# The low parts of all weights made by adding transfers of GpSimd's queue instead of VectorE subtractions

## The chip, the cores and the metric

The kernel runs on one core of one Trainium2 chip, as one program. The metric is the device time of an execution in microseconds. Engines are named TensorE (PE in rows), VectorE (DVE), ScalarE (ACT), GpSimd (POOL) and SyncE (SP, which only issues transfers here).

## The reference

One block of a network over 1024 positions of width 1024, all in float32. With `mod = silu(c) @ w_ada + b_ada` split in six:

```
h    = rmsnorm(x) * (1 + sc1) + sh1
proj = h @ w_in            # convolution branch (a_val, a_gate), z, xbc, dt
u    = silu(layernorm(causal_dwconv(a_val * sigmoid(a_gate), 31 taps))) ; out_a = u @ w_a_out
y    = ssd_scan(silu(causal_dwconv(xbc, 4 taps)), dt) ; y = rmsnorm_groups(y * silu(z)) ; out_b = y @ w_b_out
g_a, g_b = sigmoid(h @ w_gate + b_gate)
x    = x + gt1 * ((g_a * out_a + g_b * out_b) @ w_o)
h2   = rmsnorm(x) * (1 + sc2) + sh2
x    = x + gt2 * ((silu(f_gate) * f_val) @ w_down)     # f_gate, f_val: causal_dwconv(h2 @ w_up, 3 taps)
out  = rmsnorm(x)
```

## The kernel before

Channels lie on the 128 partitions and positions along the free dimension, so a tile of activations is 128x1024. Every large product is made in three: each operand is held as a high part (rounded to the type fp32r, in which TensorE takes it) and a low part (what the rounding left), and the sum is high x high + high x low + low x high. In `dense` these are L203 (`whi` with the high activations), L204 (`whi` with the low activations) and L206 (`wlo` with the high activations). A weight block is 128x1024 floats, 512 KB; it serves one product of 128 channels by 1024 positions, 48 matmuls of 512 columns. In the output projection a block serves one half of the positions only, 24 matmuls.

The program is a list of jobs. A job with a weight block takes it from `fetched`; ahead of each job `fetch_ahead` orders the blocks of this job and of the two after it. `fetch` (L165) loads the block into `raw` (two buffers, the transfer issued on SP), and `split` (L105) makes the two parts: ScalarE copies `raw` into `whi` with the rounding (L107), VectorE subtracts `whi` from `raw` into `wlo` (L98). `whi` and `wlo` have three buffers each, so the parts of block i+2 are made once the products of block i-1 are over. The first two blocks, gates 14 and 15, are loaded apart (`raw_ga`), and the four of the last group lie in buffers of their own. There are 178 blocks: 56 of `w_in`, 44 of `w_up`, 22 of `w_down`, 16 each of `w_gate`, `w_b_out` and `w_o` (each of the 8 of `w_o` twice), 8 of `w_a_out`.

In time: the inputs arrive and h is built (to 33 us); the gates, the projections of the first norm and the SSD scan in four groups (to 980 us), where VectorE also runs the 31 taps of the convolution as background work; the branch outputs `bo` and `ao` (to 1262 us), with four of the six parts of `mod` summed in the background (`ada_acc`, VectorE steps over loaded blocks of `w_ada`, whose transposes on TensorE stand in a fixed place, L234); the output projection (to 1353 us); the up- and down-projections; the last norm.

A scheduler orders the instructions of each engine from the program's order and its own estimate of when operands are ready; on the chip each engine runs its list in order, and semaphores hold an instruction until its operands and buffers are free. GpSimd runs only the powers of the norms (`rs`, L132 and L302) and issues no transfer.

Of the kernel before, what the change touches and what calls it, by code (L numbers as in the profile page):

```python
# [7 lines left out]
F32 = mybir.dt.float32  # L8
F32R = mybir.dt.float32r
AF = mybir.ActivationFunctionType  # L10
ALU = mybir.AluOpType
AX = mybir.AxisListType
PSUM = bass.MemoryType.PSUM
DRAM = bass.MemoryType.DRAM

P = 128
# [16 lines left out]
EPS = 1e-6  # L33
EPS_SSM = 1e-5

# what runs beside the SSD pieces of each group: pairs of products of the convolution branch, gates
FILL = ("ppgp", "pgpgg", "pgpgg", "pggg")

# their order: fill, z products, pieces (a, b: tokens, s: states, p: pairs of heads)
ORDER = ("fafbfspfppfpafbsfppzpzpzz",) * 3 + ("fafbspfppfpabfsppzpzpzz",)  # L40

_COLS = [
# [15 lines left out]
def block_kernel(ctx: ExitStack, tc: tile.TileContext, x, xT, par, cst, dtp, w_ada, w_in, w_dt,  # L58
                 w_gate, w_a_out, w_b_out, w_o, w_up, w_down, out):
    nc = tc.nc  # L60
    V, S, G, PE = nc.vector, nc.scalar, nc.gpsimd, nc.tensor
# [44 lines left out]
    def split(src, hi, lo):  # L106
        S.copy(hi, src)  # L107
        sub(lo, src, hi.bitcast(F32))
# [12 lines left out]
        return pars[:, o + i:o + i + n]  # L121

    def rstd_a(ps, scale, eps, name):
        """From a row ps that is the same on every partition: diagonal blocks of rsqrt(scale * ps + eps)."""
        n = ps.shape[-1] // P
        junk = small.tile([P, 4, P], F32, tag="junk", name=f"{name}_junk")[:, 0:n]
        mul(junk, ps.rearrange("p (a b) -> p a b", a=n), idb[:, 0:n])
        ms = small.tile([P, 4], F32, tag="ms", name=f"{name}_ms")[:, 0:n]
        V.tensor_reduce(ms, junk, AX.X, ALU.add)
        V.tensor_scalar(ms, ms, scale, eps, ALU.mult, ALU.add)  # L130
        rs = small.tile([P, 4], F32, tag="rs", name=f"{name}_rs")[:, 0:n]
        G.tensor_tensor(rs, ms, neghalf[:, 0:n], ALU.pow)  # L132
        dg = small.tile([P, 4, P], F32, tag="junk", name=f"{name}_dg")[:, 0:n]
        mul(dg, idb[:, 0:n], rs.unsqueeze(2).broadcast_to([P, n, P]))
        return dg

    def rstd_b(dg, name):
        """PSUM tile [P, 512]: the row on every partition."""
        dg = dg.rearrange("p a b -> p (a b)")
        ps = small_ps(f"{name}_row")[:, 0:dg.shape[-1]]  # L140
        PE.matmul(ps, ones, dg, start=True, stop=True)
        return ps
# [4 lines left out]
            PE.matmul(ps, ones, q, start=i == 0, stop=i == len(sqs) - 1)  # L147
        return ps

    # ---------------- weights: raw block -> high and low parts, loaded ahead of their use  # L150
    jobs = []
    fetched = {}

# [9 lines left out]
        return raw  # L163

    def fetch(i, raw=None, tag=None):  # L165
        make = w_tile
        if raw is None:
            ap, tag, make = jobs[i][1:]
            raw = raw_load(ap, tag)
        whi, wlo = make(f"whi_{tag}"), make(f"wlo_{tag}")  # L170
        split(raw, whi, wlo)
        fetched[i] = (whi, wlo)

    def fetch_ahead(i, n=3):
# [16 lines left out]
                fn(fetched.pop(i))  # L191

    def dense(outs, w, xs, w0=0, stride=P, after={}):
        """For each (psum, slice of the positions) in outs: psum = w.T @ xs[:, slice] over all k.
        after[k] is called behind the products of k."""
        whi, wlo = w
        nk = len(xs)
        for k in range(nk):
            a, b = xs[k]
            lh = whi[:, w0 + k * stride:w0 + k * stride + P]  # L200
            ll = wlo[:, w0 + k * stride:w0 + k * stride + P]
            for ps, sl in outs:
                PE.matmul(ps, lh, a[:, sl], start=k == 0, stop=False)  # L203
                PE.matmul(ps, lh, b[:, sl], start=False, stop=False)  # L204
            for ps, sl in outs:
                PE.matmul(ps, ll, a[:, sl], start=False, stop=k == nk - 1)  # L206
            if k in after:
                after[k]()
# [1 line left out]
    def dense2(ps, w, xs, **kw):  # L210
        dense([(ps[:, hsl(q)], hsl(q)) for q in range(2)], w, xs, **kw)

    # ---------------- modulation, first norm
    mod = cpool.tile([P, NMOD * KD], F32, name="mod")
    sc = cpool.tile([P, KD], F32, name="sc")
    th = cpool.tile([P, KD], F32, name="th")
# [20 lines left out]
            add(m, m, col("b_ada", q * KD + 4 * hh, 4))  # L237

    def row_sum(ps, col_k, raw, k):
        """One term of the sums over k; the four groups of 32 partitions hold k modulo 4."""  # L240
        kp = 32 * (k % 4)
        PE.matmul(ps[kp:kp + 32], col_k.broadcast_to([P, 32]), raw, start=k < 4, stop=k >= 4)

    def rows_to_cols(ps, dst, rows):
        """The rows ps, summed over the four groups of partitions, as columns."""
        n = dst.shape[-1]
        S.copy(rows, ps)
        pt = small_ps("rows_t")[:, 0:n * P]
        for j in range(n):
            PE.transpose(pt[:, j * P:(j + 1) * P], rows[:, j * P:(j + 1) * P], ident)  # L250
        V.tensor_reduce(dst, pt.rearrange("p (a k r) -> p a k r", a=n, k=4)[:, :, :, 0], AX.X, ALU.add)
# [66 lines left out]
    ada_rows_end(pq, 1)  # L318
    A1 = cpool.tile([P, KD], F32, name="A1")
    stt(A1, mod[:, KD:2 * KD], 1.0, col("norm1_g", 0, KD), ALU.add, ALU.mult)  # L320
    # h without the shift, for the first gates; the shift enters their bias
    halve("b_gate", 0, 16)
    for k in range(KD):
        if k < 2:
# [47 lines left out]
    cud = dram.tile([KD, P, T], F32, name="cud")  # L372
    job(first_gates_job)

    # ---------------- all projections of the first norm; SSD branch; convolution branch up to its norm
    dt, acum, mid, cd, dte = (s1.tile([P, NC, NH], F32, name=n) for n in ("dt", "acum", "mid", "cd", "dte"))
    acd = dram.tile([NH, T], F32, name="acd")

# [1 line left out]
    dts = {}  # L380

    def dt_product():
        # the sums over k lie on four groups of 32 partitions, k modulo 4
        dt_ps = dense_ps("dt_ps")
        for k in range(KD):
            kp = 32 * (k % 4)
            for h in range(2):
                PE.matmul(dt_ps[kp:kp + NH, hsl(h)], wdts[:, k], hf32[:, k, hsl(h)], start=k < 4, stop=k >= 4)
        S.copy(hf32[:, 0], dt_ps)  # L389

    def dt_softplus():
        psx = [small_ps(f"dt_tok{i}") for i in range(2)]
        for c in range(NC):
            PE.transpose(psx[c // 4][:, (c % 4) * P:(c % 4 + 1) * P], hf32[:, 0, c * CL:(c + 1) * CL], ident)
        xv, ev, zv, wv, qv = (hf32[:, 1 + n // 4, 256 * (n % 4):256 * (n % 4) + 256].rearrange(
            "p (c h) -> p c h", c=NC) for n in range(5))
        ea = hf32[:, 2, 512:512 + NH]
        S.activation(ea, dtps[:, 1], AF.Exp)
        for i in range(2):
            V.tensor_reduce(xv[:, 4 * i:4 * i + 4], psx[i].rearrange("p (c k h) -> p c h k", c=4, k=4), AX.X, ALU.add)  # L400
        add(xv, xv, dtps[:, 0].unsqueeze(1).broadcast_to([P, NC, NH]))
        # softplus(x) = max(x, 0) + log1p(e), e = exp(-|x|); log1p(e) = 2 atanh(e / (2 + e))
        stt(ev, xv, -1.0, xv, ALU.mult, ALU.max)
        S.activation(ev, ev, AF.Exp, scale=-1.0)
        V.tensor_scalar(zv, ev, 2.0, None, ALU.add)
        V.reciprocal(wv, zv)
        mul(zv, ev, wv)
        mul(wv, zv, zv)
        V.tensor_scalar(qv, wv, 1.0 / 15, None, ALU.mult)
        for n in (13, 11, 9, 7, 5, 3):  # L410
            stt(qv, qv, 1.0 / n, wv, ALU.add, ALU.mult)
        stt(qv, qv, 1.0, zv, ALU.add, ALU.mult)
        V.tensor_scalar(xv, xv, 0.0, None, ALU.max)
        stt(dt, qv, 2.0, xv, ALU.mult, ALU.add)
        dts["da"] = ev
        stt(ev, dt, -1.0, ea.unsqueeze(1).broadcast_to([P, NC, NH]), ALU.mult, ALU.mult)

    def dt_sums():
        # acum: cumulated log decay counted from the middle of its chunk
        daf = dts["da"].rearrange("p c h -> p (c h)")  # L420
        psa, psb = small_ps("acum_ps"), small_ps("tot_ps")
        PE.matmul(psa[:, 0:256], cums, daf, start=True, stop=True)
# [22 lines left out]
    acb_seq = [(hf, HG * g + q) for g in range(NG) for hf in range(2) for q in range(HG)]  # L445

    def acb_get(i):
        """acum of one head and half of the positions, on every partition."""
        for k in range(i, min(i + 3, len(acb_seq))):
            if k not in acb:  # L450
                hf, h = acb_seq[k]
                acb[k] = env["sp"].tile([P, HT], F32, tag="acb", name=f"acb{hf}_{h}", bufs=4)
                nc.sync.dma_start(acb[k], acd[h:h + 1, hsl(hf)].broadcast_to([P, HT]))
        return acb[i]

    # background work of the vector engine: the 31 taps, spread over the jobs
    bg = []

    def bg_run(n):
# [245 lines left out]
    job(lambda: merge_pools())  # L705
    job(lambda: y_raw(0))

    # ---------------- branch outputs, merge
    def merge_pools():
        sctx.close()  # L710
        env["xp2"] = ctx.enter_context(tc.tile_pool(name="xp2", bufs=8, reuse_waits="tile"))
# [69 lines left out]
            cus.append(t)  # L781

    def layer_norm():
        """Queued as background work."""
        st = {}
        put = lambda f: bg.append((0, f))

# [81 lines left out]
    for m in range(KD):  # L869
        ao_job(m)  # L870

    # output projection, residual
    gt1 = cpool.tile([P, KD], F32, name="gt1")
    A2 = cpool.tile([P, KD], F32, name="A2")
    x2 = []
# [51 lines left out]
        if m < 5:  # L927
            job(lambda m=m: norm2_b(0, 2 * m - 2, 2 * m))

    # ---------------- gated convolutional FFN  # L930
    gt2 = mod[:, 5 * KD:6 * KD]

    def ffn_pool():
# [4 lines left out]
    job(ffn_pool)  # L938

    def up_parts(m, name):  # L940
        """The two halves of a product, and what follows it."""
        def start(w):
            env["ps", m] = dense_ps(f"up_ps{m}")

# [33 lines left out]
        mk(NF + i, "v")  # L978

    def first_tiles(ms):  # L980
        """The first products: the first half of the positions before the second."""
        parts = [up_parts(m, n) for m, n in ms]
        keep = []

# [191 lines left out]
```

## Time and profile before

| | |
|---|---|
| median of 3 runs | 2103.17 us (2100.58 to 2103.53) |
| profiled execution, span from first to last instruction | 2100.7 us (the page gives no other time of it) |
| TensorE busy | 2061.3 us, 98% |
| VectorE busy | 1341.3 us, 64% |
| ScalarE busy | 766.4 us, 36% |
| GpSimd busy | 22.8 us, 1% |
| granted clock of TensorE, mean | 0.994 of 2.4 GHz |
| moved by transfers | 192.37 MB |

The busy time of TensorE counts matmuls in flight; where it is below the length of a stretch, TensorE stood still. Of the other engines, idle time costs nothing as long as nothing waits for them.

### The profile page before, as it was taken

How to read it: one execution, taken by the hardware profiler on the slowest of the kernel's cores; microseconds unless marked ns; L12 is line 12 of the kernel's file. 1: busy time of each engine (PE TensorE's matmuls, PEld its weight loads, DVE VectorE, ACT ScalarE, POOL GpSimd, SP SyncE). 2: the span in 40 equal slices, each digit the busy share in tenths (PEclk: the TensorE clock that was granted, in tenths of full speed). 3: DMA queues.
4: the chain of work that ended last, by engine and by line, in shares of the span. 5: the costliest groups of instructions: out<-in, count | busy, mean ns of one | idle time of the engine just before them, and what ended most of it. 6: DMA issues, size and time to landing. Idle time of an engine off the chain costs nothing.

```text
span 2100.7 us, 23558 instructions
## 1 busy us (share of the span) xinstructions
PE 2061.3 (98%) x9608; PEld 1664.2 (79%) x9608; DVE 1341.3 (64%) x1441; ACT 766.4 (36%) x1163; POOL 22.8 (1%) x28
## 2 busy tenths in 40 slices
PE   6999999999999999999998999999999999999997
PEld 4787787778887887788787888788888888888887
DVE  4658999999669975965886544665434434344356
ACT  5436632564237524753430323342312213122131
POOL 0000000000000000000000000000000000000000
PEclk9999999999999999999999999999999999999999
DMA  8121212232212321317385422211111111111112
GB/s 307 61 73 61 89 53 100 71 110 71 101 51 81 100 101 41 111 70 265 126 283 197 170 100 90 81 51 51 45 46 51 51 50 41 50 51 51 44 37 81
DMA packets 59964, 192.37 MB, mean 92 GB/s; under 512 B 6800, under 2 KB 10256, under 8 KB 59856
## 3 DMA queue, kind: packets, MB, share of 16 engines
q1 hardware_dynamic: 57552, 182.48, 25.5%
q10 hardware_dynamic: 2304, 8.39, 1.1%
q8 instruction: 76, 1.25, 0.2%
q14 instruction: 32, 0.26, 0.0%
HBM read 165.54 MB, written 25.30 MB: 91 GB/s over the span
## 4 chain that ended last, share of the span: by engine, by line
PE 93%; DVE 4%; DMA 2%; ACT 1%; issue 0%; POOL 0%; SPq 0%; POOLq 0%; DVEq 0%; ACTq 0%
PE up_ps L203 8%; PE up_ps L204 8%; PE up_ps L206 8%; PE xbc_ps L203 4%; PE xbc_ps L206 4%; PE xbc_ps L204 4%; PE dn_ps L203 4%; PE dn_ps L206 4%; PE dn_ps L204 4%; PE g_ps L204 3%; PE g_ps L203 3%; PE z_ps L203 3%; PE g_ps L206 3%; PE z_ps L204 3%; PE z_ps L206 3%; PE yd_ps L598 2%
## 5 line engine op out<-in xcount | busy, mean ns | idle before, releaser
L101 DVE SCALAR_TENSOR_TENSOR cu<-u,pars,cu 128x1003 f32<-128x1003 f32 (+18 forms) x240 | 300.5, 1265 | 2.3
L203 PE MATMUL up_ps<-h_hi,whi_up 128*128 128x512 f32 x704 | 274.7, 390 | 0.0
L204 PE MATMUL up_ps<-h_lo,whi_up 128*128 128x512 f32 x704 | 273.9, 389 | 0.0
L206 PE MATMUL up_ps<-h_hi,wlo_up 128*128 128x512 f32 x704 | 220.7, 389 | 0.0
L203 PE MATMUL xbc_ps<-h_hi,whi_in 128*128 128x512 f32 x384 | 153.5, 400 | 1.1 <-ACT hf L389 1.1
L203 PEld LDWEIGHTS up_ps<-h_hi,whi_up 128*128 128x128 f32 x704 | 132.1, 188 | 28.1 <-issue 0.5
L204 PEld LDWEIGHTS up_ps<-h_lo,whi_up 128*128 128x128 f32 x704 | 132.2, 188 | 27.9 <-issue 0.5
L206 PEld LDWEIGHTS up_ps<-h_hi,wlo_up 128*128 128x128 f32 x704 | 132.1, 188 | 27.4
L98 DVE TENSOR_TENSOR wlo_up<-raw_up,whi_up 128x1024 fp32r<-128x1024 f32 x44 | 53.8, 1223 | 151.3 <-ACT whi_up L107 151.0
L204 PE MATMUL xbc_ps<-h_lo,whi_in 128*128 128x512 f32 x384 | 149.7, 390 | 0.0
L107 ACT CAST whi_up<-raw_up 128x1024 fp32r<-128x1024 f32 x44 | 46.3, 1053 | 278.8 <-PE up_ps L204 137.2
L203 PE MATMUL dn_ps<-act_hi,whi_dn 128*128 128x512 f32 (+2 forms) x384 | 146.5, 382 | 1.3 <-DVE up L101 0.9
L204 PE MATMUL dn_ps<-act_lo,whi_dn 128*128 128x512 f32 (+2 forms) x384 | 143.6, 374 | 0.5 <-DVE act_lo L98 0.5
L101 DVE SCALAR_TENSOR_TENSOR x<-dn_ps,mod,x 128x1024 f32<-128x1024 f32 (+2 forms) x64 | 64.8, 1017 | 115.1 <-PE dn_ps L206 115.0
L107 ACT CAST whi_in<-raw_in 128x1024 fp32r<-128x1024 f32 x56 | 58.6, 1047 | 200.9 <-PE xbc_ps L204 72.7
L101 DVE SCALAR_TENSOR_TENSOR up<-up_ps,pars,up 128x1023 f32<-128x1023 f32 x88 | 112.6, 1279 | 14.2 <-ACT up L952 12.7
L206 PE MATMUL dn_ps<-act_hi,wlo_dn 128*128 128x512 f32 (+2 forms) x384 | 121.3, 376 | 0.0
L206 PE MATMUL xbc_ps<-h_hi,wlo_in 128*128 128x512 f32 x384 | 118.4, 390 | 0.0
L98 DVE TENSOR_TENSOR wlo_in<-raw_in,whi_in 128x1024 fp32r<-128x1024 f32 x56 | 68.4, 1221 | 63.6 <-ACT whi_in L107 63.4
L203 PE MATMUL g_ps<-h_hi,whi_ga 128*128 128x512 f32 x256 | 104.7, 409 | 2.0 <-ACT h_hi L328 1.9
L204 PE MATMUL g_ps<-h_lo,whi_ga 128*128 128x512 f32 x256 | 102.3, 400 | 0.0
L203 PE MATMUL bo_ps<-y_hi,whi_bo 128*128 128x512 f32 x256 | 102.1, 400 | 0.0
(263 smaller groups left out, 4122.6 us busy)
## 6 DMA issues: line engine op xcount, KB each, us to landing
raw_in<-in_w_in SPq DMA_DIRECT2D x56, 512.0 KB, 3.5
ada<-in_w_ada SPq DMA_DIRECT2D x48, 512.0 KB, 5.8
raw_up<-in_w_up SPq DMA_DIRECT2D x44, 512.0 KB, 3.4
acb<-acd SPq DMA_DIRECT2D x64, 256.0 KB, 3.5
raw_dn<-in_w_down SPq DMA_DIRECT2D x22, 512.0 KB, 3.4
raw_ga<-in_w_gate SPq DMA_DIRECT2D x16, 512.0 KB, 3.5
gd<-g_t ACTq DMA_DIRECT2D x16, 512.0 KB, 3.3
yd<-xs SPq DMA_DIRECT2D x16, 512.0 KB, 3.7
```

What stands on the lines that cost most here:

```text
L98: V.tensor_tensor(o, a, b, ALU.subtract)
L101: V.scalar_tensor_tensor(o, a, s, b, op0, op1)
L107: S.copy(hi, src)
L203: PE.matmul(ps, lh, a[:, sl], start=k == 0, stop=False)
L204: PE.matmul(ps, lh, b[:, sl], start=False, stop=False)
L206: PE.matmul(ps, ll, a[:, sl], start=False, stop=k == nk - 1)
L598: PE.matmul(psy[e * HD:(e + 1) * HD, i * CL:(i + 1) * CL], xdt[:, i, (2 * j + e) * HD:(2 * j + e + 1) * HD], decs[e][:, i], start=True, st ...
```

## The change

In `fetch` the subtraction of VectorE goes. ScalarE makes a second pass: it writes the negative of the high part into `wlo`. Then GpSimd's queue issues a transfer that adds the weight block to `wlo`, read a second time from DRAM (for the first two blocks from `raw_ga`). All 178 blocks take this way; `split` remains for activations. The rest of the edit takes out comments, which moves the line numbers by two.

```
     def fetch(i, raw=None, tag=None):
-        make = w_tile
+        make, ap = w_tile, None
         if raw is None:
             ap, tag, make = jobs[i][1:]
             raw = raw_load(ap, tag)
         whi, wlo = make(f"whi_{tag}"), make(f"wlo_{tag}")
-        split(raw, whi, wlo)
+        S.copy(whi, raw)
+        S.activation(wlo, whi.bitcast(F32), AF.Copy, scale=-1.0)
+        G.dma_start(wlo, raw if ap is None else ap, accum_op=ALU.add)
         fetched[i] = (whi, wlo)
```

The scheduler gives new orders. On TensorE, at the first product (gates 14 and 15, `g_ps_392` and `g_ps_393`; `ada_ps` are the steps of the shift's sum), before:

```order
L203 MATMUL g_ps_392<-h_hi_343,whi_ga_339 128x512
L203 MATMUL g_ps_393<-h_hi_343,whi_ga_347 128x512
L242 MATMUL ada_ps_0_430<-ada_0_146,sc 32x512
L204 MATMUL g_ps_392<-h_lo_344,whi_ga_339 128x512
L203 MATMUL g_ps_392<-h_hi_343,whi_ga_339 128x512
L204 MATMUL g_ps_392<-h_lo_344,whi_ga_339 128x512
L206 MATMUL g_ps_392<-h_hi_343,wlo_ga_340 128x512 x2
```

and in the changed kernel, the same place on TensorE (the gates are `g_ps_394` and `g_ps_395` there):

```order
L206 MATMUL g_ps_394<-h_lo_345,whi_ga_339 128x512
L244 MATMUL ada_ps_1_433<-ada_0_146,sc 32x512
L244 MATMUL ada_ps_0_432<-ada_1_148,sc 32x512
L244 MATMUL ada_ps_1_433<-ada_1_148,sc 32x512
L205 MATMUL g_ps_395<-h_hi_344,whi_ga_348 128x512
L206 MATMUL g_ps_395<-h_lo_345,whi_ga_348 128x512
L205 MATMUL g_ps_395<-h_hi_344,whi_ga_348 128x512
L206 MATMUL g_ps_395<-h_lo_345,whi_ga_348 128x512
L208 MATMUL g_ps_394<-h_hi_344,wlo_ga_340 128x512 x2
```

The first product with a low part (L206 before, L208 now) has moved back behind the first four products of gate 15 and three more steps of the sum; the four products and one step of gate 14 that stand ahead of these rows are the same.

On ScalarE, in the output projection (`n_q` are the squares for the second norm), before:

```order
L107 CAST whi_o_4_9033<-raw_o_4_9031 128x1024
L899 ACTIVATE n_q_1_9028<-x_1_8932 128x512
L107 CAST whi_o_5_9068<-raw_o_5_9066 128x1024
L899 ACTIVATE n_q_2_9063<-x_2_8934 128x512
L107 CAST whi_o_6_9103<-raw_o_6_9101 128x1024
L899 ACTIVATE n_q_3_9098<-x_3_8936 128x512
```

and in the changed kernel, the same blocks on ScalarE:

```order
L171 CAST whi_o_4_9133<-raw_o_4_9131 128x1024
L901 ACTIVATE n_q_1_9128<-x_1_9030 128x512
L172 ACTIVATE wlo_o_4_9134<-whi_o_4_9133 128x1024
L171 CAST whi_o_5_9169<-raw_o_5_9167 128x1024
L901 ACTIVATE n_q_2_9164<-x_2_9032 128x512
L172 ACTIVATE wlo_o_5_9170<-whi_o_5_9169 128x1024
L171 CAST whi_o_6_9205<-raw_o_6_9203 128x1024
L901 ACTIVATE n_q_3_9200<-x_3_9034 128x512
L172 ACTIVATE wlo_o_6_9206<-whi_o_6_9205 128x1024
```

The negation of each block stands behind the square of the job that ended, not right behind its cast.

## Rows read from the trace of the kernel before

**Rows 1.** The page, busy time of each engine, share of the span, instructions.

```profile
PE 2061.3 (98%) x9608; PEld 1664.2 (79%) x9608; DVE 1341.3 (64%) x1441; ACT 766.4 (36%) x1163; POOL 22.8 (1%) x28
```

**Rows 2.** Busy time by stretches; after POOL: granted clock, DMA share, GB/s.

```profile
0.00:52.00 52.00, 34.53 (x169) 21.55 (x169) 26.03 (x44) 27.14 (x39) 4.72 (x13) 0.93 0.81 311
...
33.00:41.00 8.00, 7.61 (x15) 3.22 (x16) 7.86 (x8) 8.00 (x9) 0.00 (x0) 0.61 1.03 402
...
600.00:900.00 300.00, 300.00 (x1517) 237.38 (x1516) 244.14 (x277) 161.31 (x337) 2.85 (x2) 1.00 0.25 83
...
1100.00:1150.00 50.00, 44.42 (x195) 36.45 (x194) 32.47 (x33) 4.01 (x4) 0.00 (x0) 0.93 0.65 216
...
1117.00:1121.00 4.00, 4.00 (x14) 3.52 (x15) 3.76 (x7) 0.00 (x0) 0.00 (x0) 0.50 0.45 135
...
2050.00:2101.00 51.00, 39.79 (x241) 36.85 (x239) 33.35 (x70) 9.34 (x20) 2.39 (x3) 0.90 0.24 83
```

**Rows 3.** Waits of TensorE: total us, times, longest.

```profile
PE ada_ps L234 <- DVE ada_acc L101: 5.6, 2, 4.8
```

**Rows 4.** Timeline, up-projection: start, us, engine, operation, [idle before <-releaser].

```profile
1464.30 1.05 ACT L107 CAST whi_up<-raw_up 128x1024 fp32r<-128x1024 f32 x1 [4.86 <-PE up_ps L204]
...
1465.39 1.23 DVE L98 TENSOR_TENSOR wlo_up<-raw_up,whi_up 128x1024 fp32r<-128x1024 f32 x1 [7.10 <-ACT whi_up L107]
...
1475.18 1.05 ACT L107 CAST whi_up<-raw_up 128x1024 fp32r<-128x1024 f32 x1 [3.71 <-PE up_ps L204]
...
1487.22 0.61 PE L206 MATMUL up_ps<-h_hi,wlo_up 128*128 128x512 f32 x2
```

**Rows 5.** Timeline, output projection: one block from its cast to its first use.

```profile
1290.12 1.05 ACT L107 CAST whi_o<-raw_o 128x1024 fp32r<-128x1024 f32 x1 [3.86 <-PE o_ps L204]
1291.19 0.63 ACT L899 ACTIVATE n_q<-x 128x512 f32<-128x512 f32 x1
...
1291.20 1.23 DVE L98 TENSOR_TENSOR wlo_o<-raw_o,whi_o 128x1024 fp32r<-128x1024 f32 x1
...
1301.74 0.40 PE L206 MATMUL o_ps<-mix_hi,wlo_o 128*128 128x512 f32 x1
```

**Rows 6.** Timeline, the first product (gate 14).

```profile
31.87 1.22 DVE L98 TENSOR_TENSOR wlo_ga<-raw_ga,whi_ga 128x1024 fp32r<-128x1024 f32 x1
...
32.05 1.15 ACT L328 ACTIVATE h_hi<-hf,A 128x1024 fp32r<-128x1024 f32 x1 [0.47 <-DVE A L101]
...
33.25 1.73 PE L203 MATMUL g_ps<-h_hi,whi_ga 128*128 128x512 f32 x2 [1.91 <-ACT h_hi L328]
...
34.90 1.92 PE L242 MATMUL ada_ps<-ada,sc 128*32 128x512 f32 x2
...
37.77 0.63 PE L204 MATMUL g_ps<-h_lo,whi_ga 128*128 128x512 f32 x1
...
38.19 1.06 PE L206 MATMUL g_ps<-h_hi,wlo_ga 128*128 128x512 f32 x2
```

**Rows 7.** Groups by line, L98 into low parts: count, busy us, mean ns.

```profile
L98 DVE TENSOR_TENSOR wlo_in<-raw_in,whi_in 128x1024 fp32r<-128x1024 f32 x56 | 68.4, 1221 | 63.6 <-ACT whi_in L107 63.4
...
L98 DVE TENSOR_TENSOR wlo_ao<-raw_ao,whi_ao 128x1024 fp32r<-128x1024 f32 x8 | 9.8, 1223 | 26.1 <-ACT whi_ao L107 26.1
```

**Rows 8.** Transfers by issue: count, size, median us from issue to landing.

```profile
raw_up<-in_w_up SPq DMA_DIRECT2D x44, 512.0 KB, 3.4
...
xtok<-in_x SPq DMA_DIRECT2D x8, 512.0 KB, 9.0
...
cu_in<-cud SPq DMA_DIRECT2D x8, 512.0 KB, 10.8
```

**Rows 9.** Timeline, VectorE and TensorE around the wait at 1117 us.

```profile
1106.28 1.22 DVE L98 TENSOR_TENSOR wlo_bo<-raw_bo,whi_bo 128x1024 fp32r<-128x1024 f32 x1
...
1115.62 1.28 DVE L101 SCALAR_TENSOR_TENSOR ada_acc<-ada,sc,ada_acc 128x1024 f32<-128x1024 f32 x1 [3.45 <-DMA ada<-in_w_ada]
...
1116.96 1.97 PE L234 MATMUL ada_ps<-csts,ada_acc 128*128 128x128 f32 x8 [4.80 <-DVE ada_acc L101]
```

## The prediction, made before the changed kernel was run

> **What bounds the kernel now.** I read the busy totals of the page first: TensorE is busy 2061.3 of 2100.7 us, VectorE 64%, ScalarE 36%, GpSimd 1% [rows 1]. So only 39.4 us of the span are not TensorE's, and no removal of VectorE work can be worth more than the part of them that VectorE causes. The table by stretches says where they lie [rows 2]: 17.5 us in the first 52 us (inputs arrive, h is built), 5.6 us between 1100 and 1150 us, 11.2 us in the last 51 us, and nothing from 600 to 900 us, although VectorE is at its fullest there (244 of 300 us). The table of waits of TensorE then names the largest wait that the change can touch [rows 3]: 5.6 us for `ada_acc`, a sum that VectorE makes over loaded blocks of `w_ada`. No row of that table names a weight block: all 178 of them are ready when TensorE comes to them.
>
> **How far ahead the low parts are.** In the long stages the subtraction of a block ends at 1466.6 us and the first product with that low part starts at 1487.22: 20.6 us ahead, about two products of 10.9 us (from the cast at 1464.30 to the next at 1475.18) [rows 4]. In the output projection a block feeds only half a product: the cast starts at 1290.12, the subtraction ends at 1292.43, the first use is at 1301.74, 9.3 us ahead [rows 5]. The 16 blocks of this stage and the first three of the up-projection lie within about 2 us of that. The very first block has 5.1 us: subtraction over at 33.09, first use at 38.19 [rows 6]. These three distances are what the new path has to fit into.
>
> **The change part by part.** Removed: 178 subtractions on VectorE, from 56 of `w_in` (68.4 us, 1221 ns) down to 8 of `w_a_out` (9.8 us, 1223 ns), seven groups of one duration [rows 7]: 178 x 1.22 = 217 us, 16% of VectorE's time. Nearly all of it lies beside TensorE at full work, so it is worth nothing there.
>
> Added on ScalarE: 178 negations of 128x1024. The nearest row is the cast of the same tile, 1.05 us [rows 4], so 178 x 1.05 = 187 us; ScalarE goes from 766 to 953 us, 45%. In 600 to 900 us it is busy 161 of 300 us [rows 2]; 27 blocks of 10.9 us add 28 us, 63%. The negation waits for the low buffer, which the last low product of the block three earlier frees, 0.45 us (two products) behind what the cast waits for. Behind it on ScalarE stand the evictions of PSUM and, in the SSD stage, the exponentials. A delay of 1 us there has, by the empty TensorE idle column of that stretch, never been the last thing TensorE waited for; I take 0, bounds -1 and +4 us over the stage.
>
> Added on GpSimd and the queues: 178 transfers of 512 KB that add. No transfer of GpSimd's queue and none that adds is in this trace, so T, the time from the end of the negation to the landing, is bounded: the quickest load of 512 KB by another queue, 3.4 us, and the slowest, 10.8 us, eight of them issued in a row [rows 8]. An adding transfer has to read its destination as well as its source, so I take twice the quick load, 6.8 us; while the inputs arrive, 9.0, as the loads of x have there [rows 8].
>
> The Trainium skill ("DMA: Bandwidth & Descriptors", section on the anatomy of one DMA by the gpsimd path) puts a fixed 2.0 us and bytes by 436 GB/s on such a transfer, and "Collectives: The Full Stack" (why ReduceScatter is half of AllGather) says that adding in flight halves the rate, because two sources are read: an estimate of 4.4 us. With that figure the sum below would be 1.5 us lower, since nothing waits at the start; the 512 KB loads of this trace, 3.4 us, agree with the first part (3.2 us), and nothing in it shows the second.
>
> Long stages: T may grow to about 20 us before TensorE waits. Cost 0. Output projection: on ScalarE the order is cast, square, negation; the square ends at 1291.82 (1291.19 + 0.63) [rows 5], the negation at 1292.9, and the first use is at 1301.74, so T up to 8.8 us is hidden. With 6.8 cost 0, with 10.8 see the first rival.
>
> Start: the first negation stands behind the first block of h on ScalarE, which ends at 32.05 + 1.15 = 33.20; it ends at 34.25. The transfer lands at 41.05 with T = 6.8 and at 43.25 with 9.0, against a first use at 38.19 [rows 6]. But the order of TensorE is changed with it: ahead of that product now stand 8 products and 4 steps of the shift's sum, from 33.25 on. At 0.42 us a product (37.77 to 38.19) and 1.92 us for the first step [rows 6], the other three taken as 2 us together because neighbouring steps overlap in part (a guess), they end at 33.25 + 3.4 + 1.9 + 2 = 40.55. They would only have come later, so they cost nothing. TensorE then waits 0.5 us with 6.8 and 2.7 with 9.0; I take 1.5, between 0 (T = 4) and 4.5 (T = 10.8), since the DMA engines are busy without a gap there, share 1.03, and TensorE's clock stands at 0.61 [rows 2]. The blocks of h behind the second negation come 2.1 us later, and TensorE, several blocks behind ScalarE there, does not see it.
>
> The stall at 1117 us: TensorE waits 4.80 us for `ada_acc` [rows 9]. VectorE's own chain there is step, wait for a load, step: the last step at 1115.62 waited 3.45 us for a load, and a subtraction of 1.22 us stood in the chain at 1106.28. The change takes the subtraction out, -1.2 us, and frees the raw buffer at the cast instead of behind the subtraction, so that the loads queued behind it on SP start up to 1.2 us earlier. Against that, one adding transfer per product now shares the engines. The DMA share is 0.65 at 216 GB/s [rows 2], so a full engine set moves 332 GB/s, and a transfer that reads twice 0.52 MB takes 3.2 us of it. One meets the chain for certain in the two products before the stall, perhaps two: +3.2. Net +2.0, between -2.4 and +6.4. What TensorE's clock adds is in the rows too: behind the 4.80 us stall it was granted 0.50 for 4 us [rows 2], so a longer stall costs little more, and one that vanishes gives back 2 us besides.
>
> GpSimd's powers for the norms now stand behind adding transfers in its queue, which wait for their negation. The block ahead of such a power is mostly negated by then: 0, up to +1. The last 50 us have no weight blocks: 0. The four blocks of the last group go through ScalarE ahead of an eviction, but they start as much earlier as their raw buffers are freed: 0, up to +1.
>
> Sum: 1.5 + 2.0 = +3.5 us. The page gives no time of its execution but its span, 2100.7 us, 2.5 us below the median of the runs, 2103.17; I add the sum to the median: 2106.7 us. What this measurement can tell from no change is 0.2%, 4.2 us, so the forecast stands near that edge.
>
> **The rivals.** (1) The adding transfer is slower than the output projection allows, T above 8.8 us; then it decides there. Three buffers turn once in three blocks, so each three blocks lose T - 8.8, and 19 blocks turn 6.3 times. At T = 10.8 that is 12.7 us, with 4.5 at the start and 4 at 1117 us: +21, 2124 us. At T = 15 it is 39 + 8 + 6, 2156 us. For it: nothing in the trace shows such a transfer, and loads that came eight at once took 10.8. Against: in that stage the queues carry little beside one load per 5.6 us. (2) Only the stage around 1117 us gets worse: two adding transfers meet the chain and the loads of y beside it, +6.4 and a second stall: +8, 2111 us. For it: the DMA share of 0.65 and the waits of VectorE for loads. (3) The opposite: the subtraction and the later release of the raw buffer are what makes the loads late; the stall of 4.80 us shrinks below 2, its 2 us of halved clock go, and the small waits for VectorE elsewhere (2 us) too: -6, 2097 us. Against it: the longest wait in the chain is for a load, not for VectorE. (4) ScalarE becomes late in the SSD stage, with one wait of about 1 us per group of heads and half: +8, 2111 us. Against: 63% busy at most.
>
> **How the numbers follow.** Forecast 0.48; rival 1 0.22 (0.06 of it beyond T = 12); rival 2 0.12; rival 3 0.13; rival 4 0.05. The forecast's own range is 2101 to 2110: the bounds of its two terms, not both at an end. For 8 in 10 it has to reach into rival 1 and to rival 3: 2098 to 2125. Faster by more than 0.2%: most of rival 3, 0.12. Slower: rivals 1, 2 and 4, less where they come out small, and a sixth of the forecast, 0.42. The same: 0.46.
>
> **What would show it.** Right: no wait of TensorE for a low part but at the first block; the transfer lands 5 to 8 us after its issue; VectorE's total falls to about 1124 us, ScalarE's rises to about 953; the waits for `ada_acc` come to 4 to 11 us. Wrong: rows of TensorE waiting for a DMA into `wlo_o` (rival 1), or for a transfer in the long stages, which would mean T above 20 us; a wait for `ada_acc` under 2 us (rival 3); waits of TensorE for `yd_ps` inputs between 150 and 900 us (rival 4).

## The result, and the profile after

The changed kernel takes 2128.2 us against 2102.4: ratio 1.0122, 95% interval 1.0107 to 1.0136. It is slower by 26 us where 4 were forecast and 2125 was the upper end of the range. The profiled executions, on which the following rests, differ by 28.0 us (2128.7 and 2100.7).

The busy totals and stretches of the page after [rows 1, 2 before]; columns as there. VectorE lost 199 us and ScalarE gained 176, near the 217 and 187 of the prediction (the page counts time in which two instructions of an engine overlap once; summed over the groups of instructions the differences are 216 and 187). TensorE's idle time grew from 39.4 to 61.9 us:

```profile
PE 2066.8 (97%) x9608; PEld 1666.2 (78%) x9608; DVE 1142.2 (54%) x1263; ACT 942.5 (44%) x1345; POOL 176.6 (8%) x206
```

```profile
0.00:52.00 52.00, 32.91 (x158) 19.72 (x160) 22.87 (x41) 30.16 (x42) 7.54 (x16) 0.93 0.93 332
...
600.00:900.00 300.00, 300.00 (x1509) 237.66 (x1508) 224.01 (x257) 178.86 (x355) 20.27 (x23) 1.00 0.47 121
...
982.40:1199.20 216.80, 190.81 (x814) 151.75 (x813) 123.80 (x137) 77.09 (x77) 16.37 (x18) 0.96 0.76 233
```

The last row is the branch stage, from the first product with `w_b_out` to the first with `w_a_out`. The same stretch before:

```profile
980.30:1175.10 194.80, 187.29 (x813) 150.68 (x813) 141.18 (x153) 61.40 (x61) 2.01 (x2) 0.98 0.62 215
```

It became 22.0 us longer; between 600 and 900 us TensorE is as full as before, with the share of the DMA engines up from 0.25 to 0.47. Where the rest lies is read from the start of the same product in both timelines: 2.1 us before the branch stage, 0.3 between it and the last down group, 3.2 in that group.

The waits of TensorE after, total, times, longest [rows 3 before]. In the branch stage they come to 25.9 us (`ada_ps`, `bo_ps`, `ln_sum` and two small ones), before to 7.3; the other 3.5 of the 22.0 is slower products (TensorE busy 190.8 for 187.3 us, granted clock 0.96 for 0.98; from 1132 to 1142 us, in and behind the longest wait, it was 0.50, the lower of its levels):

```profile
PE ada_ps L236 <- DVE ada_acc L101: 16.2, 3, 11.5
...
PE bo_ps L205 <- ACT y_hi L107: 4.0, 2, 2.1
PE ln_sum L801 <- DVE ln_s L95: 3.3, 1, 3.3
PE dn_ps L205 <- DVE up L101: 3.1, 1, 3.1
...
PE g_ps L208 <- DMA wlo_ga<-raw_ga: 1.8, 1, 1.8
...
PE dn_ps L208 <- DMA wlo_dn<-in_w_down: 0.4, 1, 0.4
...
PE o_ps L208 <- DMA wlo_o<-in_w_o: 0.3, 1, 0.3
```

So hardly anything waits for a low part. What is late are sums and splits over *other* loads. The loads of y that are split (`y_in`) land 9.3 us after issue at the median, before 7.3; those of the layer norm's sum (`cu_in`) 13.8, before 10.8. The queues (packets, MB, share of 16 engines) and issues (count, KB, median us to landing) [rows 8 before]:

```profile
q0 software_dynamic: 25632, 93.33, 25.5%
q1 hardware_dynamic: 57552, 182.48, 24.9%
...
ada<-in_w_ada SPq DMA_DIRECT2D x48, 512.0 KB, 8.1
...
wlo_up<-in_w_up POOLq DMA_DIRECT2D x44, 512.0 KB, 5.5
...
wlo_bo<-in_w_b_out POOLq DMA_DIRECT2D x16, 512.0 KB, 8.6
...
wlo_o<-in_w_o POOLq DMA_DIRECT2D x16, 512.0 KB, 5.6
```

25.5% of 2128.7 us over 178 transfers is 3.05 us of the whole engine set for each; SP's loads, 24.9% for 182.48 MB, come to 1.52 us for the same 512 KB. An adding transfer costs the engines two loads. The Trainium skill ("Collectives: The Full Stack", why ReduceScatter is half of AllGather) has the halved rate, for an add inside a collective; for this transfer the trace agrees. The prediction's estimate of 4.4 us to landing stands against 5.5 measured.

The ada blocks of the branch stage, after: first the steps, then VectorE's idle time for them, then issue to landing (min, median, max):

```profile
L101 DVE SCALAR_TENSOR_TENSOR ada_acc<-ada,sc,ada_acc x28: 1277/1284/1286, 1051.2 to 1163.1; 128x1024 f32<-128x1024 f32 x28
...
  DMA ada<-in_w_ada: 48.8, 16
...
DMA to landing us min/median/max: 3.4/6.9/13.4
```

and before:

```profile
L101 DVE SCALAR_TENSOR_TENSOR ada_acc<-ada,sc,ada_acc x28: 1275/1284/1286, 1044.3 to 1141.5; 128x1024 f32<-128x1024 f32 x28
...
  DMA ada<-in_w_ada: 14.8, 11
...
DMA to landing us min/median/max: 3.6/4.7/7.2
```

No step is slower; 16 of the 32 wait for their load (11 before), 34 us more in all. The chain of four sums takes 114 us (1050.4 to 1164.4) instead of 99, while the program hands it out over six products, 65 us. The longest wait, where it ends [rows 9 before]:

```profile
1127.05 1.28 DVE L101 SCALAR_TENSOR_TENSOR ada_acc<-ada,sc,ada_acc 128x1024 f32<-128x1024 f32 x1 [4.27 <-DMA ada<-in_w_ada]
...
1129.60 1.28 DVE L101 SCALAR_TENSOR_TENSOR ada_acc<-ada,sc,ada_acc 128x1024 f32<-128x1024 f32 x1 [1.26 <-DMA ada<-in_w_ada]
...
1133.78 1.28 DVE L101 SCALAR_TENSOR_TENSOR ada_acc<-ada,sc,ada_acc 128x1024 f32<-128x1024 f32 x1 [2.89 <-DMA ada<-in_w_ada]
...
1138.05 1.28 DVE L101 SCALAR_TENSOR_TENSOR ada_acc<-ada,sc,ada_acc 128x1024 f32<-128x1024 f32 x1 [2.99 <-DMA ada<-in_w_ada]
...
1139.39 1.97 PE L236 MATMUL ada_ps<-csts,ada_acc 128*128 128x128 f32 x8 [11.49 <-DVE ada_acc L101]
```

Four steps in a row each wait for a load, and TensorE, which takes its instructions in order, stands behind the last.

### The profile page after: what moved, and what is told of

Same layout as the page of the kernel before. It is cut to its first block, busy times and chain, and to the rows that moved or that the text cites. A ratio compares the mean times of both kernels' runs of the same rounds, so it can differ in the third digit from the quotient of the medians.

```text
span 2128.7 us, 23954 instructions
## 1 busy us (share of the span) xinstructions
PE 2066.8 (97%) x9608; PEld 1666.2 (78%) x9608; DVE 1142.2 (54%) x1263; ACT 942.5 (44%) x1345; POOL 176.6 (8%) x206
## 3 DMA queue, kind: packets, MB, share of 16 engines
q0 software_dynamic: 25632, 93.33, 25.5%
q1 hardware_dynamic: 57552, 182.48, 24.9%
## 4 chain that ended last, share of the span: by engine, by line
PE 82%; DMA 7%; DVE 6%; ACT 2%; issue 2%; POOL 0%; SPq 0%; POOLq 0%; DVEq 0%; ACTq 0%
PE up_ps L208 7%; PE up_ps L206 7%; PE up_ps L205 7%; PE dn_ps L205 4%; PE dn_ps L208 4%; PE dn_ps L206 4%; PE xbc_ps L205 3%; PE xbc_ps L206 3%; PE xbc_ps L208 3%; DMA ada<-in_w_ada 3%; PE g_ps L208 3%; PE g_ps L205 3%; PE g_ps L206 3%; PE z_ps L205 2%; PE z_ps L208 2%
## 5 line engine op out<-in xcount | busy, mean ns | idle before, releaser
L101 DVE SCALAR_TENSOR_TENSOR cu<-u,pars,cu 128x999 f32<-128x999 f32 (+19 forms) x240 | 300.9, 1264 | 2.4
L206 PE MATMUL up_ps<-h_lo,whi_up 128*128 128x512 f32 x704 | 273.9, 389 | 0.0
L208 PE MATMUL up_ps<-h_hi,wlo_up 128*128 128x512 f32 x704 | 220.6, 389 | 0.0
L206 PEld LDWEIGHTS up_ps<-h_lo,whi_up 128*128 128x128 f32 x704 | 132.1, 188 | 28.1 <-issue 0.5
L208 PEld LDWEIGHTS up_ps<-h_hi,wlo_up 128*128 128x128 f32 x704 | 132.2, 188 | 27.3
L206 PE MATMUL xbc_ps<-h_lo,whi_in 128*128 128x512 f32 x384 | 149.5, 389 | 0.0
L206 PE MATMUL dn_ps<-act_lo,whi_dn 128*128 128x512 f32 (+2 forms) x384 | 144.0, 375 | 0.0
L208 PE MATMUL dn_ps<-act_hi,wlo_dn 128*128 128x512 f32 (+2 forms) x384 | 121.9, 378 | 0.4 <-DMA wlo_dn<-in_w_down 0.4
L208 PE MATMUL xbc_ps<-h_hi,wlo_in 128*128 128x512 f32 x384 | 118.5, 390 | 0.0
L173 POOL DMA_DIRECT2D wlo_in<-in_w_in x56 | 49.1, 876 | 651.8 <-ACT wlo_in L172 567.4
L206 PE MATMUL g_ps<-h_lo,whi_ga 128*128 128x512 f32 x256 | 102.7, 401 | 0.0
L206 PE MATMUL bo_ps<-y_lo,whi_bo 128*128 128x512 f32 x256 | 101.4, 397 | 1.2 <-DVE y_lo L98 1.1
```

The lines of the kernel that those rows point to most:

```text
L101: V.scalar_tensor_tensor(o, a, s, b, op0, op1)
L173: G.dma_start(wlo, raw if ap is None else ap, accum_op=ALU.add)
```

## The experiments

Theory C: the adding transfers compete with the other loads for the DMA engines. Rival S: ScalarE's negations make the splits of y late. The table gives each run's ratio and, from the profiled executions, how many us each stretch is longer than before (start of the first product of a weight in either timeline): up to the branch stage, the branch stage, the products of `w_a_out`, from there to the last down group, that group.

```
run              ratio  interval           to branch  branch   w_a_out  to last  last
changed kernel   1.0122 1.0107 to 1.0136      2.1      22.0      0.0      0.3     3.2
sub_bo           1.0032 1.0021 to 1.0044      5.9      -1.7      0.0     -0.2     2.6
add_bo           1.0086 1.0070 to 1.0103      0.1      19.2      0.0      0.0     0.0
neg_act_sum_dve  1.0028 1.0019 to 1.0038      1.4       1.8      0.0      0.4     2.3
extra_bo         1.0118 1.0101 to 1.0135     -2.8      22.8      0.0      0.0     0.0
extra_one        1.0056 1.0039 to 1.0073     -0.1      12.9      0.0      0.0     0.5
plain_bo         1.0028 1.0017 to 1.0039     -1.7       5.2      0.0      0.0     0.0
after_bg4        1.0162 1.0147 to 1.0177      4.5      26.0      1.6     -0.2     2.5
after_half       1.0139 1.0123 to 1.0154      2.4      17.0      0.0      4.9     3.1
after_late       1.0050 1.0033 to 1.0067      4.2      -4.2      4.8     -0.1     2.8
before_mp10      1.0003 0.9993 to 1.0014     -0.7      -7.5      7.3      0.0    -0.1
before_bg4       1.0010 1.0001 to 1.0020      0.1      -3.2      1.7      0.0     0.0
before_half      0.9987 0.9977 to 0.9996     -0.1      -4.8      0.0     -0.1     0.0
before_late      0.9967 0.9955 to 0.9978      1.1     -10.4      2.9      0.0     0.0
sub_edges        1.0001 0.9991 to 1.0010      1.5      -0.2      0.0     -0.2     0.0
edges_half       1.0008 0.9998 to 1.0019      0.7      -5.4      0.0      3.0     0.0
before_both      0.9957 0.9940 to 0.9974     -1.4     -10.6      1.6      0.0    -0.1
```

The first column is not worth much: kernels whose first products are made as before lie between -2.8 and 1.5 in it.

**Which blocks (sub_bo, add_bo).** In the changed kernel's `fetch`:

```diff
+        if tag[:2] != "bo":          # sub_bo; add_bo has == "bo"
         S.activation(wlo, whi.bitcast(F32), AF.Copy, scale=-1.0)
         G.dma_start(wlo, raw if ap is None else ap, accum_op=ALU.add)
+        else: sub(wlo, raw, whi.bitcast(F32))
```

> Subtraction on VectorE for the 16 blocks of the branch projection (w_b_out) alone, adding transfers for the other 162. Against the kernel before, the changed one lost 22.0 us between the first product of that stage and the first of w_a_out, 2.1 before it, 0.5 in the output projection and 3.1 in the last down group. Theory C (transfers compete: each adding transfer takes the DMA engines for 3.05 us, and the chain of ada_acc sums pays it load by load) and theory S (ScalarE's negations make the splits of y late) both say that the 22 us go: about 2108 us, ratio 1.003, and VectorE's wait for ada loads back from 48.8 to about 15 us. If the loss came from the stages ahead of it (buffers or queues that fall behind), the time would stay above 2120.

> The opposite: adding transfers for the 16 blocks of w_b_out alone, subtraction for the other 162. C: the stage alone carries the loss, about +18 to +22 us, 2120 to 2125 us, ratio 1.0085 to 1.0105, with ada loads landing in about 6.9 us (4.7 before). S: the same. If the loss needs the other stages too (the 8 blocks of w_a_out that come next, or what falls behind earlier), it is below 10 us.

Both came out as expected, 2107.7 and 2120.7 us. The 16 transfers of `w_b_out` alone make the loss. In sub_bo VectorE's wait for ada loads is that of before:

```profile
  DMA ada<-in_w_ada: 14.1, 12
...
DMA to landing us min/median/max: 3.6/4.6/7.2
```

**Negation or transfer (neg_act_sum_dve, extra_bo, extra_one, plain_bo).**

```diff
 # neg_act_sum_dve, in place of the transfer      # plain_bo, w_b_out only
+ add(wlo, wlo.bitcast(F32), raw)                 + G.dma_start(wlo, ap)
 # extra_bo, before's fetch, behind the split; extra_one: one transfer of 736 columns
+ G.tensor_copy(env["extra"][:, 0:1], whi[:, 0:1].bitcast(F32))
+ for e in range(2):
+     G.dma_start(env["extra"], ap[:, e * 512:(e + 1) * 512], accum_op=ALU.add)
```

> All 178 low parts: the negation stays on ScalarE, but the sum with the raw block is made by VectorE; no adding transfer. ScalarE has the work of the changed kernel, VectorE that of the kernel before, the queues that of the kernel before. C: the 22 us of the branch stage go, because no transfer competes; 2101 to 2107 us, ratio 0.9995 to 1.002. S: they stay, 2118 to 2128 us. The last down group, where ScalarE's eviction stood behind a cast and a negation, should keep 1 to 2 us of its 3.1 by either.

2105.9 us: the branch stage loses 1.8 us, not 22. S falls as the explanation of the 22 us. The time is inside the expected range, the ratio of 1.0028 above its upper end of 1.002; ScalarE's negations and what they delay cost about 5 us, half of it in the last group.

> The kernel before with its subtractions, and beside them, for 13 of the 16 blocks of w_b_out, the same 512 KB as two adding transfers of 256 KB into a tile that nobody reads, issued by GpSimd when the high part is cast. No low part depends on them and ScalarE does nothing more. C: most of the loss appears all the same, +12 to +22 us, 2114 to 2124 us, ratio 1.0057 to 1.0105. S: nothing, 2102 us.

2126.1 us, above the upper end. Its waits show why that is no clean proof of C; the first row was 0.9 us before:

```profile
PE ln_row L141 <- DVE ln_dg L92: 12.2, 2, 6.5
...
PE ada_ps L238 <- DVE ada_acc L101: 10.0, 3, 5.7
```

The powers of the layer norm run on GpSimd, and its queue stood waiting for the first of two transfers onto one tile: 6.98 us ahead of the issue at 1029.16, with the power behind it at 1029.73.

```profile
1029.16 0.87 POOL L175 DMA_DIRECT2D extra<-in_w_b_out  x1 [6.98 <-DMA extra<-in_w_b_out]
1029.73 1.37 POOL L132 TENSOR_TENSOR ln_rs<-ln_ms,neghalf 128x4 f32<-128x4 f32 x1
```

This is the queueing that the prediction had looked for in the real change and that is not there (`ln_row` 0.9 us after).

> As the run with extra transfers that nobody reads, but one adding transfer of 368 KB a block instead of two of 256 KB onto one tile, so that GpSimd never waits for its own landing. In that run TensorE's wait for the layer norm's powers on GpSimd was 12.2 us (0.9 before), and that part was the queueing of GpSimd, not the sharing of the DMA engines. Here that wait should be about 1 us and the wait for ada_acc 8 to 14 us: +6 to +14 us, 2107 to 2115 us, ratio 1.003 to 1.007. If without the queueing nothing is left, 2101 us, sharing alone would not explain the loss.

2112.9 us, as expected. GpSimd still waited three times for a landing of its own, but TensorE's wait for the powers is back at 0.8 us. Without that queueing, transfers on which nothing depends cost 12.9 us in the stage: 5.9 more of waiting for `ada_acc`, 4.1 at the splits of y and the layer norm's sum, the rest slower products (TensorE busy 190.4 for 187.3 us):

```profile
PE ada_ps L237 <- DVE ada_acc L101: 11.5, 3, 5.5
...
PE ln_row L141 <- DVE ln_dg L92: 0.8, 1, 0.8
```

> Low parts of w_b_out made by a transfer of GpSimd's queue that overwrites instead of adding (the sum with the negated high part is left out there), all other low parts by subtraction: only adding differs from the run that had adding transfers for these 16 blocks (ratio 1.0086). If adding is what doubles the time on the DMA engines (3.05 us against 1.52 for a load of this size), the loss is about half or less, +4 to +10 us, ratio 1.002 to 1.005. If the queue itself is the dear part (its descriptors, or that it is another queue), the loss stays, +16 to +20 us.

2106.9 us: overwriting costs 5.2 us in the stage, adding 19.2. The queue is not the dear part, adding is: GpSimd's queue took 1.2% of the engines' 2104.6 us for 16 overwriting transfers and 2.2% of 2120.4 for 16 adding ones, 1.6 and 2.9 us each. Engine time alone does not give the size: with 25 us added (overwriting), 30 (extra_one, 1.4% of 2113.9; its transfers were 14, not the 13 expected) and 47 (add_bo) the stage grew by 5.2, 12.9 and 19.2. The length of the chain of sums goes better with it: 101.5, 107.4 and 111.1 us against 99.3 before. The run with overwriting has no subtraction on VectorE in this stage and extra_one has all of them; what that is worth was not tested.

**The chain (after_bg4, before_bg4, before_mp10, before_half, after_half).** If sharing makes each load later, is it that the chain has two buffers, that it is handed out too fast, or that the engines are simply full?

```diff
-            bg_run(6)
+            bg_run(4)                     # after_bg4, before_bg4
-        ... name="mp", bufs=11 ...
+        ... name="mp", bufs=10 ...        # before_mp10
 # after_half, before_half: mp 9, and for the ada blocks
+            for h in range(2):
+                st[k, h] = env["mp"].tile([P, HT], F32, tag="ah", name=f"ada_{q}_{k}_{h}", bufs=5)
+                nc.sync.dma_start(st[k, h], w_ada[k, :, q * D + h * HT:q * D + (h + 1) * HT])
...
+            for h in range(2):
+                ada_step(st["acc"][:, hsl(h)], st.pop((k, h)), k)
```

> The changed kernel, but each product of the branch projection carries 4 pieces of the work beside it instead of 6 (layer norm first, then the four ada_acc chains), so the 32 ada loads spread over about 100 us instead of 65. If the loss is the chain of loads paid one by one because it is packed too closely for the loads' longer landing (theory C, mechanism chain), most of the 22 us go: 2107 to 2114 us, ratio 1.003 to 1.006, and VectorE's wait for ada loads stays but TensorE's wait for ada_acc falls from 16.2 to under 5 us. If the loss is DMA throughput over the whole stage (theory C, mechanism volume: 0.76 of the engines' time is used), spreading gives little: over 2120 us.

> The same edit on the kernel before: 4 pieces instead of 6 beside each product. Mechanism chain: its own wait for ada_acc (5.6 us) and the slow clock behind it go, 2094 to 2098 us, ratio 0.996 to 0.998. Mechanism volume: no change, 2102 us. If the later end of the chain meets the flush ahead of w_a_out's products, it is slower, 2105 to 2115.

Both missed what the chain would give: 2135.0 us, slower than with 6, and 2103.1. With 4 pieces the layer norm ends later, the chain starts later (1092 us, not 1050) and ends at 1204, behind the point ahead of `w_a_out` where all of it must be done; four waits for `ada_acc` come to 21.3 us.

> The kernel before with one buffer less in the pool (10 instead of 11) that the running sums, the ada_acc and the ada loads share, so that once eight sums are held one ada load is in flight instead of two. Theory chain: with two buffers a step costs about half of a load's landing plus the step, (4.7 + 1.28) / 2 = 3.0 us, 32 steps 96 us (98 in the trace); with one it costs the whole, 6.0 us, at least for the steps behind the eighth sum: the chain grows by 40 to 95 us and TensorE loses 30 to 90 us, 2132 to 2192 us. Theory volume (the engines' time over the stage decides): same bytes, 2101 to 2106 us.

A plain miss, 2102.2 us. With one buffer less, part of the chain moved behind the stage (its last step ends at 1226 us), which freed 7.5 us there and cost 7.3 in the next. So the run did not slow the loads' overlap as meant, and two buffers as the limit remain unshown.

> The kernel before with the ada blocks loaded and summed in halves of 256 KB, in five buffers of half a block of their own (2.5 blocks in flight instead of 2, and a buffer is free after half a step). Theory chain: a block costs about 2 x (4 + 0.7) / 5 = 1.9 us instead of 3.0, so the chain keeps up with the products and the wait for ada_acc (5.6 us) and the slow clock behind it go: 2094 to 2099 us, ratio 0.9965 to 0.9985. Theory volume: 2101 us.

> The changed kernel with the same halves in five buffers. The adding transfers and all bytes stay. Theory chain: the landing of a load stays longer, but more of them overlap: 10 to 16 of the 22 us of the branch stage come back, 2111 to 2118 us, ratio 1.0045 to 1.008; VectorE's wait for ada loads from 48.8 to under 25 us. Theory volume: nothing comes back, 2124 to 2130 us.

On the kernel before the halves bring 3.4 us: 2098.0, inside the expected range, with a ratio of 0.9987 just short of it. On the changed kernel VectorE's wait for ada loads halves as expected (23.8 us), yet only 5.0 of the 22 come back, and 3.1 us of waits for `wlo_o` appear in the next stage: 2130.8 us, no gain, a miss. More loads in flight do not help enough where the chain is still handed out over 65 us. By their times alone these runs speak for volume: four of the five came out in or within 1.1 us of its range. The next pair decides.

**The pace (after_late, before_late).**

```diff
-            bg_run(6)
+            bg_run(6 if hk == 0 and m < 5 else 3)
...
-    job(lambda: bg_run(len(bg)))
     job(u_split)
     for m in range(KD):
         ao_job(m)
+        if m == 1: job(lambda: bg_run(len(bg)))
```

> The changed kernel with 6 pieces beside each of the first five products (the layer norm), 3 beside each of the other eleven, and what is left behind the second product of w_a_out instead of ahead of the first. A chain of 36 pieces that needs 113 us then meets 12 products (131 us), where 4 pieces a product (98 us) were still too quick for it. Theory chain: the waits for ada_acc fall from 16.2 (21.3 with 4 pieces) to under 6 us; the layer norm's part of the loss (6 to 7 us by the third product) stays: 2108 to 2116 us, ratio 1.003 to 1.007. Theory volume: over 2120 us.

> The kernel before with the edit of after_late alone (6 pieces of side work for five products, then 3, the rest behind the second product of w_a_out). Theory pace: its chain needs 98 us and has 131, so the wait for ada_acc (5.6 us) and the slow clock behind it go in the branch stage; 2 to 5 us may come back in the w_a_out products, as after_late lost 4.8 there: 2096 to 2101 us, ratio 0.997 to 1.0. If the edit itself is worth 15 us or more whatever the transfers do, 2087 us or less.

2110.9 us, as expected, and 2095.3, 0.7 below its range. In after_late the adding transfers run, the engines are fuller in the branch stage than in the changed kernel, VectorE waits for ada loads nearly as long (47.5 us for 48.8), and TensorE no longer waits for `ada_acc` at all. The branch stage of after_late:

```profile
984.50:1175.10 190.60, 185.28 (x806) 149.00 (x804) 112.15 (x125) 74.33 (x75) 16.01 (x18) 0.99 0.82 256
```

So the engines were not too full for the stage's bytes (0.82 here, 0.76 in the changed kernel). What cost TensorE most of its time is that the sums, made late by the sharing, stood too early in its order. The edit takes 26.2 us off the branch stage of the changed kernel and 10.4 off that of the kernel before; 4.8 and 2.9 come back in the products of `w_a_out`. It does not make the transfers free: with this pace in both kernels they still cost 6.2 us in the branch stage (3.2 of it TensorE's wait for the layer norm's sum, 2.2 slower products), where they had cost 22.0. In the whole span it is 14.2 us (2108.6 and 2094.4).

**The account, and the best version (sub_edges, edges_half, before_both).** sub_edges has the condition of sub_bo for the gates, `w_b_out` and the last down group; edges_half adds the halves to it; before_both is the kernel before with halves and pace.

> Subtraction on VectorE where TensorE was seen to lose time: the 16 gates (the first two at the start), the 16 blocks of w_b_out, the 4 of the last down group; adding transfers for the other 142. If the three places are the whole account (start 3 to 6 us, branch 22, last group 3): the time of before, 2099 to 2105 us, ratio 0.999 to 1.0015. If adding transfers in the long stages cost or gain something that the waits don't show, it lies outside.

> The same mix, with the ada blocks in halves and five buffers, which took the kernel before from 2101.4 to 2098.0 us. If VectorE's relief by 142 subtractions is worth anything, this is faster than 2098; I expect 2095 to 2101 us, ratio 0.997 to 1.0, no different from before_half.

> The kernel before with both edits to the ada chain (halves in five buffers, 3 pieces a product and the rest behind the second product of w_a_out), no adding transfer. Halves alone left 3.0 us of wait for ada_acc; with the slower pace none is left: 2094 to 2099 us, ratio 0.9965 to 0.9985.

sub_edges came to 2102.0 against 2102.1 us: with the three places on VectorE again, 142 adding transfers and 142 subtractions fewer are worth nothing. edges_half missed (2104.6): beside the gain of the halves it waits 2.8 us for `wlo_o`, in the output projection that rival 1 spoke of. Its profiled execution took 2101.2, so where the other 3.4 us of the median lie is not seen. before_both, with no adding transfer, is the fastest: 2092.9 us, ratio 0.9957, ahead of both kernels and 1.1 us below its range.

## Why the prediction was wrong

- **Removed subtractions, worth nothing in the long stages.** Right: 300.00 of 300 us of TensorE before and after; sub_edges shows it at 1.0001. The negations, put at 0 as well, cost 1.4 us up to the branch stage in neg_act_sum_dve, inside the spread of that column.
- **T, 6.8 us taken, up to 8.8 hidden in the output projection.** Right: the transfers land 5.6 us after issue there at the median, TensorE waits 0.3 us. In the branch stage they take 8.6, more than the 5 to 8 foretold, and nothing waits for them. Rival 1 did not decide: its 2124 us lies near the measured time by coincidence, its place was the wrong one.
- **Start, +1.5 us.** Near: the wait for the first low part is 1.8 us (3.1 to 4.8 in the four other runs with this start, one of them beyond the bound of 4.5). The 1.5 was a value between the waits for T = 6.8 and 9.0. Of these 9.0 was the right one: the two transfers land 9.2 us after issue at the median, and TensorE goes on at 43.38 us, where the prediction had 43.25 for the landing. The wait is 1.8 and not 2.7 because the products ahead ended at 41.6, 1 us later than the guess of 40.55.
- **The stall at 1117 us, +2.0, which failed.** The step said: "One meets the chain for certain in the two products before the stall, perhaps two: +3.2. Net +2.0, between -2.4 and +6.4." The mechanism (adding transfers share the engines with the loads of `ada_acc`) and the 3.2 us of engine time were right (3.05 measured). The size was not: I charged one transfer against one wait, at the stall alone. The chain has 32 loads, with a median landing of 6.9 us for 4.7, and VectorE's wait for them grew by 34.0 us. TensorE saw 10.6 us of that at `ada_acc`; 8 more came at the splits of y and the layer norm's sum, whose loads were late as well, and 3.5 of slower products: 22.0. Rival 2 named this place and carried the same error (+8). The stage as a whole would have warned of it: 16 transfers of 3.05 us are 49 us of engine time in 195 us in which the engines were at 0.62. It would not have given the size.
- **The last down group, 0, up to +1, also failed.** It cost 3.2 us. The last eviction of the up-projection (ScalarE's reading of a product out of PSUM) stands behind the cast and the negation of the last block on ScalarE; its input was ready at 2060.07 (the last product of `up_ps`, 2059.68 + 0.39), and it began at 2063.11:

```profile
2061.07 1.05 ACT L171 CAST whi_dn<-raw_dn 128x1024 fp32r<-128x1024 f32 x1 [3.73 <-DMA raw_dn<-in_w_down]
2062.15 1.06 ACT L172 ACTIVATE wlo_dn<-whi_dn 128x1024 fp32r<-128x1024 f32 x1
2063.11 1.19 ACT L954 ACTIVATE up<-up_ps,pars 128x1024 f32<-128x1024 f32 x1
...
2067.08 0.58 PE L205 MATMUL dn_ps<-act_hi,whi_dn 128*128 128x384 f32 x1 [3.14 <-DVE up L101]
```

  One us is the late load, two are cast and negation. How much of it the transfers make is open: neg_act_sum_dve, without them, loses 2.3 us here, but its sums on VectorE delay the loads too.
- **GpSimd's powers, 0 to +1.** Right, TensorE waits 0.9 us for the layer norm's as before; extra_bo shows what it costs when GpSimd does wait (12.2).

## What to carry to other kernels

Here work moved from an engine with slack to the DMA engines was paid where *other* loads are on the path. For each stage, set the engine time added beside the share in use, and ask which chain consumes loads one by one and where TensorE's order waits for its end. Count an adding transfer as two loads (3.05 us of engine time for 1.52). And look first at the place of a chain that a stage makes late: three pieces a product and a later deadline gave back more (26.2 and 10.4 us of the stage) than deeper buffers did (5.0 and 4.8), with or without the transfers.

## Not expected of the hardware

A load under the competition of one adding transfer per product lands in 6.9 us at the median, 13.4 at worst (4.7 and 7.2 before), although the engines are at 0.76 on average: the mean share says little about a single landing. And the order of cost was not by bytes written: 16 overwriting transfers cost the stage 5.2 us, 16 adding ones of the same size 19.2, with about twice the engine time.
